# A chunked linear-attention scan: running sums placed behind the step, value rows copied on the chip, weight pieces offered twice as often

## The chip, the cores and the metric

The kernel runs on one core of a Trainium2 chip. A core has five engines that run their own instruction streams in order and meet only at semaphores: PE (matrix products, with PEld loading the stationary operand), DVE (vector), ACT (activation functions and scaled copies), POOL (GpSimd) and SP (which here only issues DMA transfers). The metric is the device time of one execution in microseconds (us): for the kernel before, the median of three runs is 2766.99 us (2765.91 to 2770.10).

## The reference, cut to what matters

Two layers of a hybrid backbone. Each layer has modulation vectors (`silu(c) @ w_ada`), three parallel token mixers merged by sigmoid gates, and a gated feed-forward part. The change touches the first mixer (a delta-rule scan in two directions, six heads of 64), and the modulation and gate products that are computed beside it.

```python
def _rwkv_step(S, inp):
    r, w, k, v, a, b = inp
    sa = jnp.einsum('bhij,bhj->bhi', S, a)
    S = S * w[:, :, None, :] + sa[..., None] * b[:, :, None, :] + v[..., None] * k[:, :, None, :]
    return S, jnp.einsum('bhij,bhj->bhi', S, r)
...
mod_lat = (jax.nn.silu(c) @ w_ada[l] + b_ada[l])[:, None, :]
...
gA, gB, gC = jnp.split(jax.nn.sigmoid(gate_u), N_BRANCH, axis=-1)
m = gA * (yA @ p['w_branch_a']) + gB * (yB @ p['w_branch_b']) + gC * (yC @ p['w_branch_c'])
```

## The kernel before, in words

Weights are split into a high and a low float32r part (L183 on ACT, L184 on DVE) and each dense product is three passes over them. Each layer goes through: projections for the scan (`rwkv_project`), the scan (`rwkv_scan`), the other mixers (Fourier and attention, `mixers`), the merge and the feed-forward part. In the profile the scan of layer 0 lies at about 205 to 600 us, the mixers of layer 0 behind it to about 890 us, and the scan of layer 1 at about 1780 to 2120 us.

The scan is cut into 12 chunks of 64 tokens for both directions at once. A chunk n has a **preparation** and a **step**.

- The preparation, `prep(n)`, reads the chunk's tile `X` (four transfers, L991 and L992, from `rwx` and `rws`), makes the running sum of the log decays (`cum`, L1006, one DVE instruction), five exponentials of it on ACT (L1013 to L1017), the scaled operands `BK` and `AR` (L1024 to L1030), their products (`f`), the masks (`MA`, `MY`), and then inverts a triangular matrix in eight rounds (`inverse`, tiles `i...`, L1087 to L1139): each round is a PE product followed by DVE or ACT work that the next product waits for. Its result is `TT`. At the end GpSimd copies `AR` into `MA` (L1060).
- The step, `step(n)`, is the serial part: product with the state `SV`, copy `Rh` (L1153, DVE), product with `TT`, copy into `UV` (L1160 on DVE, L1161 on ACT), product with `Bn`, `St` (L1173) and the new state `SV` (L1175, one half on DVE and the other on GpSimd). The outputs `y` are products of `SV` and `UV`.
- `SV` and `UV` both hold, in one half of their partitions, the value rows of the chunk. Before, both are filled from the array `v_tok` in memory by four transfers each (L978 for `SV`, three buffers; L999 for `UV`, three buffers). `X` has two buffers (`XB`).

SP issues all these transfers and the weight tiles (`wr`, three buffers in rotation, L191 for gate weights, L245 for modulation weights) in one order; a transfer whose buffer is still in use holds back all that stand behind it.

**Background work.** The products of the gates (`L688`, bank `w`, one buffer; ACT reads them out at L693) and the modulation parts (`ada_part`, L258: eight small products per part in four pieces of 512 KB of weights, then L261, four transposes at L265 and a reduction at L268) are not part of the scan. `Background.after` is called behind each small product chain of the scan and issues some of that work there, counted in planned microseconds (`due`). While the scan runs (`side`), a modulation part can be advanced by one piece (`aside`, bank `a`, its next piece loaded ahead) at each point where the gate stream yields 0.0: at the end of each of its two parts (512 and 256 columns), and, where `MID[l]` is true, also halfway through each. What is left of layer 0's modulation parts when its scan ends is put between the remaining gates (`mix`) and runs in the mixers phase from the `fill` calls, in the bank `w` that the gates use, without loading ahead.

The order of instructions on each engine is fixed when the program is built: a list scheduler with a simulated timeline places each instruction when its inputs are ready by its own estimate; `tc.issue_after(x)` keeps an instruction behind instruction x in it.

Of the kernel before, what the change touches and what calls it, by code (L numbers as in the profile page):

```python
# [11 lines left out]
F32 = mybir.dt.float32  # L12
# [3 lines left out]
ALU = mybir.AluOpType  # L16
# [49 lines left out]
MFILL, AFILL = 2.5, 0.3  # L66
FIRST = ((12, 2.0), (8, 3.0))
MORE = False
XB, UB = 2, 3
MID = (False, True)  # L70
FILL = (1.0, 0.8)
PRE = (12.0, 24.0)
CUTS = dict(
# [9 lines left out]
def hybrid_backbone_kernel(ctx: ExitStack, tc: tile.TileContext, A, out, dbg=None):  # L83
    nc = tc.nc
    V, S, P, TE = nc.vector, nc.scalar, nc.gpsimd, nc.tensor
# [21 lines left out]
    def pss(tag="s"):  # L107
        return banks[tag].tile([128, 512], F32, tag=tag, name=tag)
# [6 lines left out]
    def C(name, n=None):  # L115
        o = COFF[name]
        w = dict(CCOLS)[name] if n is None else n
        return cst[:, o:o + w]
# [45 lines left out]
    v_tok = dram.tile([T, 2, 3, 64], F32, name="v_tok")  # L164
# [506 lines left out]
    def gate_part(l, it, W, hH, hL, streams, pool):  # L671
# [3 lines left out]
        for a, b in streams:  # L675
# [8 lines left out]
            else:  # L684
                WH, WL = W
                for n, (w, X) in enumerate(((WH, hH), (WL, hH), (WH, hL))):
                    for k in range(8):
                        TE.matmul(ps, lhsT=w[:, k, :], rhs=X[k][:, a:b], start=(k == 0 and n == 0), stop=(k == 7 and n == 2))  # L688
                        if (n, k) != (2, 7):
                            yield (b - a) / 2400  # L690
                        if MID[l] and (n, k) == (1, 3):
                            yield 0.0
# [249 lines left out]
    def rwkv_scan(l, last, pool, fill):  # L942

        hs = (slice(0, 64), slice(64, 128))
# [27 lines left out]

        def state(n):

            SV = pool.tile([128, 2, 6, 64], F32, tag="SV", name="SV", bufs=3)
            for d, c in enumerate(chunks(n)):
                for p in range(2):
                    nc.sync.dma_start(out=SV[hs[1 - p], p, 3 * d:3 * d + 3, :], in_=v_tok[c * 64:c * 64 + 64, p])  # L978
            return SV


        def chunks(n):
            return (8 + n, 11 - n) if n < 4 else (n - 4, 11 - n)

        def load(n):
            ch = chunks(n)
            need_y = not (last and n < 4)
            X = pool.tile([128, 5, 2, 192], F32, tag="X", name="X", bufs=XB)
            for d in range(2):
                w = 2 if need_y else 1  # L990
                nc.sync.dma_start(out=X[:, 2:5, d], in_=rwx[d, ch[d]].rearrange("p w c t -> p w (c t)"))  # L991
                nc.sync.dma_start(out=X[:, 0:w, d], in_=rws[ch[d], :, 0:w].rearrange("p w c t -> p w (c t)"))  # L992
            return X

        def values(n):
            UV = pool.tile([128, 2, 6, 64], F32, tag="UV", name="UV", bufs=UB)
            for d, c in enumerate(chunks(n)):
                for p in range(2):
                    nc.sync.dma_start(out=UV[hs[1 - p], p, 3 * d:3 * d + 3, :], in_=v_tok[c * 64:c * 64 + 64, p])  # L999
            return UV  # L1000

        def prep(n, X):
            need_y = not (last and n < 4)
            w = 128 if need_y else 64
            cum = pool.tile([128, 2, 192], F32, tag="cum", name="cum", bufs=1)
            V.tensor_tensor_scan(out=cum.rearrange("p d x -> p (d x)"), data0=C("seq"), data1=X[:, 4].rearrange("p d x -> p (d x)"),  # L1006
                                 initial=0.0, op0=ALU.mult, op1=ALU.add)
            G = Gs[n % 2]
            I = X[:, 4]
            gc = pool.tile([128, 6], F32, tag="gc", name="gc", bufs=4)  # L1010
            c = 0.5 * DECAY_C
# [129 lines left out]

        def step(n, SV, UV, pk):
            AR, MY, Bn, TT, gc, WA = pk
# [3 lines left out]
            ps, run = pss("st"), Run()  # L1147
            for u in range(6):
                for p in range(2):
                    i = run(TE.matmul, ps[hs[p], u * 64:(u + 1) * 64], lhsT=WA[:, p, u, :], rhs=SV[:, p, u, :], start=True, stop=True)  # L1150
            fill(i)
            Rh = pool.tile([128, 384], F32, tag="Rh", name="Rh", bufs=1)
            V.tensor_copy(Rh, ps[:, 0:384])  # L1153
            ps, run = pss("st"), Run()
            for u in range(6):
                for p in range(2):
# [5 lines left out]
            if n < 11:  # L1162
                gb = gc.unsqueeze(2).to_broadcast([128, 6, 64])
                Sg = pool.tile([128, 6, 64], F32, tag="Sg", name="Sg", bufs=1)
                for p in range(2):
                    P.tensor_tensor(out=Sg[hs[p]], in0=SV[hs[p], p], in1=gb[hs[p]], op=ALU.mult)
                ps, run = pss("st"), Run()
# [8 lines left out]
            if need_y:  # L1176
                ps = pss("st")
# [3 lines left out]
                for u in range(6):  # L1181
                    for p in range(2):
                        o = ps[hs[p], u * 64:(u + 1) * 64]
                        m1 = run(TE.matmul, o, lhsT=SV[:, p, u, :], rhs=AR[:, u, 2 - 2 * p, :], start=True, stop=False)
                        for q in prev:
# [12 lines left out]
                    S.dma_start(out=y_dram[d, :, :, ch[d] * 64:ch[d] * 64 + 64].rearrange("c p t -> p c t"), in_=yt[:, d])  # L1198
            return SV1

        ld = [load(0), load(1)]
        SV = state(0)
        for p in range(2):
            P.memset(SV[hs[p], p], 0.0)
        uv = [values(0), values(1)]
        pk = [prep(0, ld[0])]
        ld.append(load(2))
        uv.append(values(2))
        pk.append(prep(1, ld[1]))
        for n in range(12):  # L1210
            if n + 3 < 12:
                ld.append(load(n + 3))
            SV = step(n, SV, uv[n], pk[n])
            if n + 3 < 12:
                uv.append(values(n + 3))
            if n + 2 < 12:
                pk.append(prep(n + 2, ld[n + 2]))

    def rwkv_out(l, last, pool, fill):

# [39 lines left out]
    for k in range(KD):  # L1260
        x = xp.tile([128, T], F32, name=f"x{k}")
# [24 lines left out]
    for l in range(DEPTH):  # L1286
# [8 lines left out]
        with ExitStack():  # L1295
# [28 lines left out]
            def fill(us=MFILL):  # L1324
                bg.run(us)
# [27 lines left out]
        with ExitStack() as es:  # L1353
            for c in range(8):
                x = xp.tile([128, T], F32, name=f"x{c}")
# [4 lines left out]
            with ExitStack() as e2:  # L1360
                tp = near(e2, l, f"mt{l}")
                for c in range(8):
                    acc = None
                    for x in (2, 1, 0):
                        t = tp.tile([128, T], F32, tag=f"t{x}", name=f"t{x}", bufs=2)
                        nc.sync.dma_start(out=t[:, ar], in_=t_dram[x, c][:, ar])
                        ps = dense(A[("w_ba", "w_bb", "w_bc")[x]][l, c], len(yX[x][0]), yX[x][0], yX[x][1], streams)
# [169 lines left out]
```

## Time and profile before

| | |
|---|---|
| median of three runs | 2766.99 us |
| the profiled execution | 2763.33 us |
| its span, first to last instruction | 2761.6 us |
| PE busy | 2580.6 us (93%) |
| DVE, ACT, POOL busy | 1474.6, 1076.6, 209.7 us |
| mean granted TensorE clock | 0.975 |
| largest DMA queue (SP's) | 278.66 MB, 32.5% of 16 engines' span |

A busy PE is not a PE at its peak, but where it is idle or at the lower clock, time is lost that nothing else can give back, since PE has work left over in every stage. So the stages are read by PE's idle time and granted clock first, then by what PE waited for there, and then by what that engine waited for.

### The profile page before, as it was taken

The numbers are of one execution on the slowest core, as the hardware profiler recorded it, in microseconds if no ns is written. First come the engines' busy times: TensorE is split into PE (matmuls) and PEld (weight loads), VectorE is DVE, ScalarE is ACT, GpSimd is POOL, SyncE is SP. The second block draws the span as 40 slices with busy tenths as digits, with TensorE's granted clock in tenths as the row PEclk, the third lists the DMA queues.
The fourth block names the chain that finished last, engine by engine and source line by source line (L and its number), as shares of the span: only waits on it lengthen the run. The fifth ranks groups of instructions, "written<-read, shape, count | busy, mean of one in ns | idle before, by whom it ended". The sixth has DMA issues, their size and how long they took to land.

```text
span 2761.6 us, 56820 instructions
## 1 busy us (share of the span) xinstructions
PE 2580.6 (93%) x24016; PEld 2062.0 (75%) x24016; DVE 1474.6 (53%) x2965; ACT 1076.6 (39%) x1914; POOL 209.7 (8%) x268
## 2 busy tenths in 40 slices
PE   6998998997899999999999999998898899899999
PEld 4866776775776887888888877666666668878778
DVE  6444545434446765445354564445564768755455
ACT  4353333332445253222222344544343564533333
POOL 0121121100010000000000001302220000000000
PEclk9999998998999999999999999999999999999999
DMA  6365443356441641221212254765444417333334
GB/s 264 93 176 173 132 137 108 119 190 205 133 139 42 183 122 48 60 69 55 68 49 74 61 170 109 234 196 154 134 134 148 130 50 220 108 92 90 98 95 123
DMA packets 168947, 344.18 MB, mean 125 GB/s; under 512 B 33618, under 2 KB 84436, under 8 KB 168692
## 3 DMA queue, kind: packets, MB, share of 16 engines
q1 hardware_dynamic: 132532, 278.66, 32.5%
q0 software_dynamic: 10944, 36.58, 5.0%
q10 hardware_dynamic: 25216, 25.30, 2.7%
q8 instruction: 190, 3.11, 0.5%
q14 instruction: 65, 0.53, 0.1%
HBM read 278.60 MB, written 61.87 MB: 123 GB/s over the span
## 4 chain that ended last, share of the span: by engine, by line
PE 67%; DMA 5%; DVE 5%; ACT 2%; issue 2%; SPq 1%; ACTq 0%; POOL 0%; DVEq 0%; POOLq 0%
PE mm L220 44%; PE w L688 9%; PE mm L567 2%; DMA wr<-in_w_ada 2%; PE r L595 2%; PE s L584 1%; PE st L957 1%; PE i L957 1%; DVE wl L184 1%; PE mm L394 1%; DMA X<-rwx 1%; PE a L258 1%; PE w L258 1%; PE s L871 1%; DMA raw<-m_dram 1%
## 5 line engine op out<-in xcount | busy, mean ns | idle before, releaser
L183 ACT ACTIVATE wh<-wr 128x1024 fp32r<-128x1024 f32 (+4 forms) x334 | 302.0, 906 | 373.7 <-PE mm L220 272.1
L184 DVE TENSOR_TENSOR wl<-wr,wh 128x1024 fp32r<-128x1024 f32 (+3 forms) x332 | 342.8, 1034 | 59.4 <-ACT wh L183 56.9
L220 PE MATMUL mm<-fH,wh 128*128 128x512 f32 (+1 forms) x1072 | 223.9, 357 | 10.3 <-DVE ab L232 7.2
L231 DVE SCALAR_TENSOR_TENSOR ab<-mm,prm,ab 128x511 f32<-128x511 f32 (+1 forms) x132 | 86.8, 658 | 262.3 <-ACT ab L229 262.3
L220 PE MATMUL mm<-fH,wl 128*128 128x512 f32 (+1 forms) x1072 | 220.3, 353 | 0.0
L220 PE MATMUL mm<-fL,wh 128*128 128x512 f32 (+1 forms) x1072 | 219.6, 352 | 0.0
L688 PE MATMUL w<-hH,wh 128*128 128x512 f32 (+1 forms) x760 | 189.0, 385 | 22.4 <-ACT gt L693 21.0
L220 PEld LDWEIGHTS mm<-fH,wh 128*128 128x128 f32 x1072 | 178.1, 191 | 41.7 <-issue 6.4
L220 PEld LDWEIGHTS mm<-fH,wl 128*128 128x128 f32 x1072 | 175.8, 189 | 29.6
L220 PEld LDWEIGHTS mm<-fL,wh 128*128 128x128 f32 x1072 | 175.4, 188 | 29.5
L688 PE MATMUL w<-hL,wh 128*128 128x512 f32 (+1 forms) x760 | 184.4, 374 | 0.0
L220 PE MATMUL mm<-gH,wh 128*128 128x512 f32 (+1 forms) x568 | 174.5, 346 | 10.0 <-ACT wh L183 4.4
L688 PE MATMUL w<-hH,wl 128*128 128x512 f32 (+1 forms) x760 | 174.6, 364 | 2.7 <-issue 2.7
L220 PE MATMUL mm<-gH,wl 128*128 128x512 f32 (+1 forms) x568 | 175.4, 348 | 1.1 <-DVE wl L184 0.9
L688 PEld LDWEIGHTS w<-hH,wh 128*128 128x128 f32 x760 | 128.6, 197 | 63.2 <-ACT gt L693 29.6
L1255 DVE SCALAR_TENSOR_TENSOR x<-mm,mod,x 128x256 f32<-128x256 f32 (+1 forms) x136 | 80.1, 607 | 173.1 <-PE mm L220 172.2
L220 PE MATMUL mm<-gL,wh 128*128 128x512 f32 (+1 forms) x568 | 171.5, 343 | 0.0
L229 ACT ACTIVATE ab<-mm,prm 128x768 f32<-128x768 f32 (+1 forms) x88 | 69.9, 795 | 217.9 <-PE mm L220 217.9
L688 PEld LDWEIGHTS w<-hL,wh 128*128 128x128 f32 x760 | 128.6, 195 | 25.1 <-issue 4.1
L688 PEld LDWEIGHTS w<-hH,wl 128*128 128x128 f32 x760 | 128.1, 192 | 24.7 <-issue 3.3
L220 PEld LDWEIGHTS mm<-gH,wh 128*128 128x128 f32 x568 | 97.1, 188 | 29.6 <-ACT wh L183 10.4
L693 ACT ACTIVATE gt<-w 128x512 f32<-128x512 f32 x99 | 51.4, 519 | 161.7 <-PE w L688 143.6
(387 smaller groups left out, 4649.8 us busy)
## 6 DMA issues: line engine op xcount, KB each, us to landing
wr<-in_w_up SPq DMA_DIRECT2D x88, 512.0 KB
wr<-in_w_ada SPq DMA_DIRECT2D x80, 512.0 KB
wr<-in_w_g SPq DMA_DIRECT2D x48, 512.0 KB
wr<-in_w_out SPq DMA_DIRECT2D x32, 512.0 KB
wr<-in_w_dn SPq DMA_DIRECT2D x48, 320.0 KB
X<-rwx SPq DMA_DIRECT2D x48, 288.0 KB
wr<-in_w_rw SPq DMA_DIRECT2D x24, 512.0 KB
wr<-in_w_dn SPq DMA_DIRECT2D x32, 384.0 KB
```

The source lines that it names most:

```text
L183: S.activation(out=H, in_=raw, func=AF.Copy)
L184: e.tensor_tensor(out=L, in0=raw, in1=H.bitcast(F32), op=ALU.subtract)
L220: TE.matmul(ps[:, a:b], lhsT=W[:, k, :], rhs=X[k][:, a:b], start=(k == 0 and n == 0), stop=(k == kt - 1 and n == 2))
L229: S.activation(out=o[:, a:b], in_=ps[:, a:b], func=AF.Identity, scale=w[1])
L231: V.scalar_tensor_tensor(out=o[:, a + 1:b], in0=ps[:, a:b - 1], scalar=w[0], in1=o[:, a + 1:b], op0=ALU.mult, op1=ALU.add)
L258: TE.matmul(ps[32 * i:32 * i + 32], lhsT=cs32[:, k, :], rhs=w[:, k - k0], start=(k < 4), stop=(k >= 4))
L567: TE.matmul(ps[:, a:b], lhsT=qT[:, h, t * 128:(t + 1) * 128], rhs=kT[:, h, a:b], start=True, stop=True)
L595: TE.matmul(po[64 * p:64 * p + 64, 0:128], lhsT=Vn[:, j, h * 64:(h + 1) * 64], rhs=pts[p][:, j * 128:(j + 1) * 128], start=(j == kts[0]), ...
L688: TE.matmul(ps, lhsT=w[:, k, :], rhs=X[k][:, a:b], start=(k == 0 and n == 0), stop=(k == 7 and n == 2))
L693: S.activation(out=t[:, a:b], in_=ps, func=AF.Tanh if it[0] == "g" else AF.Copy, scale=0.5 if it[0] == "g" else 1.0)
L957: self.i = f(*a, **k)
L1255: V.scalar_tensor_tensor(out=x[:, a:b], in0=ps[:, a:b], scalar=mod[l][:, j, c, s:s + 1], in1=x[:, a:b], op0=ALU.mult, op1=ALU.add)
```

## The change

Four edits in the scan and two numbers.

- `cum` of chunk n+2 is issued behind `Rh` of step n (`issue_after`); the sums of chunks 0 and 1 stay free.
- `UV` gets its value rows from `SV` by two GpSimd copies per chunk (64 partitions x 384 elements) in place of four transfers; it has two buffers in place of three.
- `SV` has four buffers in place of three.
- `MID` is true for layer 0 too, as it was for layer 1.

```diff
-XB, UB = 2, 3
-MID = (False, True)
+XB, UB = 2, 2
+MID = (True, True)
...
-            SV = pool.tile([128, 2, 6, 64], F32, tag="SV", name="SV", bufs=3)
+            SV = pool.tile([128, 2, 6, 64], F32, tag="SV", name="SV", bufs=4)
...
-        def values(n):
+        def values(SV):
             UV = pool.tile([128, 2, 6, 64], F32, tag="UV", name="UV", bufs=UB)
-            for d, c in enumerate(chunks(n)):
-                for p in range(2):
-                    nc.sync.dma_start(out=UV[hs[1 - p], p, 3 * d:3 * d + 3, :], in_=v_tok[c * 64:c * 64 + 64, p])
+            for p in range(2):
+                P.tensor_copy(UV[hs[1 - p], p], SV[hs[1 - p], p])
             return UV
...
-        def prep(n, X):
+        def prep(n, X, behind=None):
...
-            V.tensor_tensor_scan(out=cum.rearrange("p d x -> p (d x)"), data0=C("seq"), data1=X[:, 4].rearrange("p d x -> p (d x)"),
-                                 initial=0.0, op0=ALU.mult, op1=ALU.add)
+            with tc.issue_after(behind.ins) if behind else ExitStack():
+                V.tensor_tensor_scan(out=cum.rearrange("p d x -> p (d x)"), data0=C("seq"), data1=X[:, 4].rearrange("p d x -> p (d x)"),
+                                     initial=0.0, op0=ALU.mult, op1=ALU.add)
...
-            V.tensor_copy(Rh, ps[:, 0:384])
+            rhs[0] = V.tensor_copy(Rh, ps[:, 0:384])
...
-        uv = [values(0), values(1)]
...
-            SV = step(n, SV, uv[n], pk[n])
-            if n + 3 < 12:
-                uv.append(values(n + 3))
+            SV = step(n, SV, values(SV), pk[n])
             if n + 2 < 12:
-                pk.append(prep(n + 2, ld[n + 2]))
+                pk.append(prep(n + 2, ld[n + 2], rhs[0]))
```

Three places in the new order, each before and after. The first is DVE in layer 0 about the fourth step (chunk 3, `Rh_4109` before and `Rh_4113` after). Before, the running sum `cum_5113` there is that of chunk 7, and it stands ahead of the step:

```order
L1101 TENSOR_TENSOR iX_3848<-i0_3853,iDX_3805 128x192
L1006 SCALAR_TENSOR_TENSOR cum_5113<-cst_75,X_4535 128x384
L1103 TENSOR_TENSOR iNX_3806<-i0_3898,iX_3848 128x6x32
L1137 COPY TT0_1870<-i1_3597 32x3x32
L1105 STREAM_TRANSPOSE iXt_3849<-iNX_3806 128x192
L1137 COPY TT0_1870<-i1_3597 32x3x32
L1027 TENSOR_TENSOR AR0_1877<-X_4077,G0_1873 128x6x64
L1153 COPY Rh_4109<-st_4087 128x384
```

After, the sum behind the same step is that of chunk 5 (`cum_4188`), and the operands `BK` and `AR` that are made from it follow at once, in part ahead of the step's next copy, `UV`:

```order
L1153 COPY Rh_4113<-st_4095 128x384
L1006 SCALAR_TENSOR_TENSOR cum_4188<-cst_75,X_3609 128x384
L1090 TENSOR_TENSOR iD0_3800<-iF_3795,cst_75 128x192
L1093 TENSOR_TENSOR iE_3802<-iF_3795,cst_75 128x192
L1091 STREAM_TRANSPOSE iDt_3801<-iD0_3800 128x192
L1092 TENSOR_TENSOR iDX_3803<-iD0_3800,cst_75 128x6x32
L1024 TENSOR_TENSOR BK_4196<-X_3609 128x6x64
L1026 TENSOR_TENSOR BK_4196<-X_3609 128x6x64
L1160 COPY UV_4087<-st_4115 64x384
```

So the sums stand two chunks ahead of the step in place of four.

The second place is SP at the start of layer 0's scan, where the tiles `X` of chunks 0 and 1 and the first value rows are fetched. Before:

```order
L991 DMA X_1889<-rwx_114 128x3x192
L992 DMA X_1889<-rws_113 128x2x192
L991 DMA X_1889<-rwx_114 128x3x192
L245 DMA wr_2020<-in_w_ada 128x1024
L992 DMA X_1889<-rws_113 128x2x192
L991 DMA X_1894<-rwx_114 128x3x192
L992 DMA X_1894<-rws_113 128x2x192
L991 DMA X_1894<-rwx_114 128x3x192
L992 DMA X_1894<-rws_113 128x2x192
L978 DMA SV_1899<-v_tok_115 64x192 x4
L999 DMA UV_1906<-v_tok_115 64x192 x3
```

After, with the same names but for their numbers:

```order
L991 DMA X_1893<-rwx_114 128x3x192
L992 DMA X_1893<-rws_113 128x2x192
L991 DMA X_1893<-rwx_114 128x3x192
L245 DMA wr_1844<-in_w_ada 128x1024
L191 DMA wr_1849<-in_w_m 128x1024
L245 DMA wr_2115<-in_w_ada 128x1024
L992 DMA X_1893<-rws_113 128x2x192
L991 DMA X_1898<-rwx_114 128x3x192
L992 DMA X_1898<-rws_113 128x2x192
L991 DMA X_1898<-rwx_114 128x3x192
L992 DMA X_1898<-rws_113 128x2x192
L978 DMA SV_1903<-v_tok_115 64x192 x2
```

The transfers into `UV` are gone, and three weight tiles in place of one stand ahead of the last part of the first `X`.

The third place is PE in the mixers phase of layer 0, behind a gate's last product of 256 columns. Before, a modulation part (L258, its transposes L265) stands between this gate and the next:

```order
L688 MATMUL w<-hL_156,wh 128x256
L416 MATMUL s<-cst,sq 128x1 x6
L258 MATMUL w<-wr,cs_102 32x512 x8
L265 MATMUL w<-cst,row 128x128 x4
L688 MATMUL w<-hH_141,wh 128x512
```

After, the attention's own products (L394) stand there, and the next gate comes without a part between:

```order
L688 MATMUL w<-hL_155,wh 128x256
L688 MATMUL w<-hL_156,wh 128x256
L394 MATMUL mm<-mh,cH 128x384
L394 MATMUL mm<-mh,cL 128x384
L394 MATMUL mm<-ml,cH 128x384
L394 MATMUL mm<-mh,cH 128x384
```

Counted over the whole order of PE: of the 12 modulation parts in the background of layer 0, 6 run in the scan and 6 in the mixers phase before; after, 10 and 2, and the mixers phase has 9 gates in place of 8. Layer 1 has all its 8 parts in its scan in both.

## Rows read from the trace of the kernel before

**Rows 1.** The page: busy time, share and instructions of each engine.
```profile
PE 2580.6 (93%) x24016; PEld 2062.0 (75%) x24016; DVE 1474.6 (53%) x2965; ACT 1076.6 (39%) x1914; POOL 209.7 (8%) x268
```
**Rows 2.** Busy time by stretch: length, engines (instructions), PE clock, DMA share, GB/s.
```profile
205.00:260.00 55.00, 45.66 (x415) 33.95 (x418) 22.28 (x47) 17.82 (x47) 11.28 (x20) 0.88 0.61 181
260.00:480.00 220.00, 196.81 (x4353) 156.41 (x4344) 113.24 (x273) 81.49 (x211) 38.24 (x44) 0.97 0.44 131
480.00:580.00 100.00, 98.81 (x2112) 77.66 (x2109) 42.99 (x107) 34.32 (x82) 16.93 (x20) 0.97 0.35 109
674.00:780.00 106.00, 90.45 (x514) 70.56 (x514) 43.35 (x125) 44.02 (x67) 4.42 (x9) 0.90 0.45 143
1800.00:2040.00 240.00, 217.57 (x4609) 159.14 (x4609) 131.81 (x310) 98.57 (x247) 39.02 (x45) 0.96 0.52 160
2040.00:2117.00 77.00, 72.99 (x1675) 53.88 (x1669) 37.41 (x92) 27.24 (x64) 16.57 (x18) 1.00 0.43 124
```
**Rows 3.** Who PE waited for, 260 to 480 us: total, times, longest.
```profile
PE w L688 <- ACT gt L693: 9.4, 2, 7.0
PE i L954 <- DVE iX L1101: 4.1, 2, 3.3
```
**Rows 4.** Instructions in order of time, 346 to 359 us: SP, DVE, ACT, PE.
```profile
346.73 2.90 SPq L999 DMA_DIRECT2D UV<-v_tok  x4
349.93 0.55 SPq L991 DMA_DIRECT2D X<-rwx  x1
...
356.31 0.96 DVE L1006 TENSOR_TENSOR_SCAN cum<-cst,X 128x384 f32<-128x384 f32 x1 [2.65 <-DMA X<-rwx]
...
357.35 0.36 ACT L1013 ACTIVATE X<-cum 128x192 f32<-128x192 f32 x1 [5.99 <-DVE cum L1006]
...
358.40 0.21 PE L954 MATMUL i<-iX,iQ 32*32 32x32 f32 x1 [2.60 <-ACT iQ L1125]
```
**Rows 5.** Line 1006, whole span: DVE idle before it, until what; total, times.
```profile
  DMA X<-rwx: 84.5, 19
```
**Rows 6.** Who SP's queue waited for, 200 to 610 us: total, times, longest.
```profile
SPq L978 <- PE st L957: 55.3, 7, 12.9
```
**Rows 7.** Lines 999, 1060, 1027: count, duration min/median/max in ns, first and last start.
```profile
L999 SPq DMA_DIRECT2D UV<-v_tok x96: 444/593/1980, 230.2 to 2060.9; - x96
...
L1060 POOL COPY MA<-AR x48: 496/505/722, 275.1 to 2112.3; 64x384 f32<-64x384 f32 x48
...
L1027 DVE TENSOR_TENSOR AR<-X,G x24: 526/550/1335, 228.7 to 2041.7; 128x384 f32<-128x384 f32 x24
```
**Rows 8.** Start of layer 0's scan, in order of time: SP, PE.
```profile
208.52 0.59 SPq L991 DMA_DIRECT2D X<-rwx  x1
223.49 0.34 SPq L245 DMA_DIRECT2D wr<-in_w_ada  x1
...
245.13 0.25 PE L954 MATMUL i<-iD,iDt 32*32 32x32 f32 x1 [4.43 <-DVE iDt L1091]
```
**Rows 9.** Who PE waited for, 674 to 780 us: total, times, longest.
```profile
PE w L258 <- DMA wr<-in_w_ada: 10.7, 4, 4.5
```
**Rows 10.** PE in order of time: last pieces of two modulation parts, mixers of layer 0.
```profile
710.97 1.92 PE L258 MATMUL w<-wr,cs 128*32 128x512 f32 x4 [2.54 <-DMA wr<-in_w_ada]
...
743.25 1.05 PE L258 MATMUL w<-wr,cs 128*32 128x512 f32 x4 [1.96 <-DMA wr<-in_w_ada]
```
**Rows 11.** Who PE waited for, 1800 to 2117 us: total, times, longest.
```profile
PE w L688 <- ACT gt L693: 6.0, 3, 5.7
PE a L258 <- DMA wr<-in_w_ada: 4.4, 3, 2.5
```
**Rows 12.** Lines 1153, 1025, 1139 in layer 1's scan: as in Rows 7.
```profile
L1153 DVE COPY Rh<-st x12: 545/557/558, 1856.2 to 2117.2; 128x384 f32<-128x384 f32 x12
L1025 ACT ACTIVATE BK<-BK x12: 515/524/527, 1792.1 to 2063.1; 128x384 f32<-128x384 f32 x12
L1139 ACT ACTIVATE TT<-i x24: 241/242/243, 1850.0 to 2113.5; 32x96 f32<-32x96 f32 x24
```

More of the change, by code (lines that the diff above doesn't have):

```diff
@@ L1199, in step @@
             return SV1
+        rhs = [None]
         ld = [load(0), load(1)]
@@ L1204, in rwkv_scan @@
             P.memset(SV[hs[p], p], 0.0)
-        uv = [values(0), values(1)]
         pk = [prep(0, ld[0])]
         ld.append(load(2))
-        uv.append(values(2))
         pk.append(prep(1, ld[1]))
```

## The prediction

> **What bounds the kernel now.** I read the page first: PE is busy for 2580.6 of 2761.6 us [rows 1], so about 181 us of idle PE is all that any rearrangement can win, beside what the clock takes. The change leaves PE's products as they are and moves them, so the question is where in the three stages it touches PE stands idle or slow. The view of busy time by stretch gives that [rows 2]. In the middle of layer 0's scan (260 to 480 us) PE is idle for 220 - 196.8 = 23.2 us; in the 100 us behind it, where no running sum is left to make, for 1.2 us. In layer 1 it is idle for 240 - 217.6 = 22.4 us up to 2040 us, and for 77 - 73.0 = 4.0 us behind. In the mixers of layer 0, from 674 to 780 us, it is idle for 106 - 90.5 = 15.5 us and the granted clock is 0.90, that is, part of this stretch runs at 1.2 and not 2.4 GHz.
>
> Then the waits. In layer 0's scan PE's longest waits are for ACT to empty the gate bank (9.4 us in two waits, one of 7.0) and for DVE and ACT inside the inversion [rows 3]. These engines are not busy (DVE 113 of 220 us, [rows 2]), so something holds them in their order. Rows in order of time show what: SP spends 2.90 us on four `UV` transfers, and only then issues `X`, at 349.93; DVE has the running sum of that `X` next in its order and stands idle for 2.65 us until 356.31; ACT waits for the sum 5.99 us; the small ACT copy that PE needs stands behind, and PE is idle for 2.60 us [rows 4]. DVE waits for `X` in this way 19 times, 84.5 us in all [rows 5]. SP itself was held back before: its `SV` transfers wait 55.3 us for PE's products of an older step, because `SV` has three buffers [rows 6].
>
> **The change part by part.** I sum against the profiled execution, 2763.3 us.
>
> *Running sums behind the step, four `SV` buffers, no `UV` transfers.* The order shows the sum two chunks ahead of the step in place of four. Its `X` then takes a buffer that came free about two steps earlier, while SP loses 96 transfers of 0.59 us each (57 us of issue, [rows 7]) and the wait on the third `SV` buffer. So `X` has landed when the sum comes up, and the 84.5 us of DVE idle should all but go. PE gets back only its own part. From both sides: nothing, if other waits take their place; at most the idle down to the quiet rates, 23.2 - 2.2 x 1.2 = 20.6 us in layer 0 and 22.4 - 240 x 4.0 / 77 = 9.9 us in layer 1 [rows 2]. The quiet stretches have fewer preparations in flight, so I stay below: 15 us and 8 us. The clock of these stretches is 0.97 and 0.96, at most 6.6 and 9.6 us of full-speed time; the quiet stretch of layer 1 has 1.00, that of layer 0 only 0.97. I take 2 and 4 us. Scans: -29 us.
>
> *What this costs.* Behind `Rh` DVE now has the sum (0.96 us), two `BK` and two `AR` products, with a wait for ACT's exponentials, partly ahead of the step's `UV` copy. That is some 4 to 5 us on the step's serial path where before it was spread; it is covered as long as PE has gate products between, which the order still places there. With a chunk less of lead the inversion's rounds stand closer together, and each round too close costs PE a fraction of a microsecond. Not shown in any row: between 0 and the whole gain; I take 3 us.
>
> *Copies by GpSimd.* 48 copies of 64 x 384, like line 1060's at 0.505 us [rows 7]: 24 us of an engine that is busy for 209.7 us [rows 1]. They need no time on the path, since the values of chunk n+2 are copied while step n+1 is still to come. But DVE's `AR` product, 550 ns at the median, took up to 1335 ns [rows 7], 0.79 us more, and GpSimd is the engine that works at the same time on the same tiles. Between 0 and 48 x 0.79 = 38 us of DVE time; most copies will meet no such product, and DVE has as much idle as busy time, so I take 2 us for PE.
>
> Beside that stands a rule of the Trainium skill, "SBUF — State Buffer", section "Who interferes with whom": a DVE instruction with two SBUF inputs and a GpSimd instruction that reads SBUF exclude each other, and the later one blocks until the earlier ends. It speaks against the copies, and this trace agrees with it as far as the 550 and 1335 ns go. By it a copy would hold such a DVE instruction for its own 0.5 us at most, 24 us of DVE time for all 48, within the bounds above; the sum stays.
>
> *Modulation parts halfway through layer 0's gates.* By the order, 4 of 6 parts leave the mixers phase for the scan and one gate goes the other way. PE's work is the same in sum. In the mixers a part is loaded piece by piece without loading ahead: the four parts between 674 and 780 us cost four waits for the last piece, 10.7 us [rows 9]. The stall also costs clock: the last piece took 1.92 us behind one such wait and 1.05 us behind another [rows 10], a factor of 1.83, near that of the two levels, and 0.90 over 106 us is at most 10.6 us of full-speed time [rows 2]. The four parts that leave are these, as the order has the gates at their places without them; the first two, at 604 to 655 us, stay. Between 0 (if attention's own chain sets the pace there) and 15.5 + 10.6 = 26 us; I take the 10.7 us and 3 us of clock. Mixers: -14 us.
>
> In the scan a part is loaded one piece ahead. Layer 1 shows the price: 8 parts, 4.4 us of waits [rows 11], so 0.55 us each, 2 us for four more.
>
> *The start of layer 0's scan.* Here the change adds to a queue. Before, SP stood from 208.5 to 223.5 us in front of one modulation tile, which waits for a buffer, and the rest of the first `X` came behind it [rows 8]; PE then waited 4.43 us for the first inversion [rows 8] and was idle for 55 - 45.7 = 9.3 us in this stretch [rows 2]. After, three tiles stand there, each waiting for a buffer that PE's products release. Two more issues are 0.7 us and two more tiles of 512 KB at the 181 GB/s of this stretch [rows 2] 5.8 us, if nothing overlaps; from 1 to 7 us, I take 3.
>
> Sum: -29 + 3 + 2 - 14 + 2 + 3 = -33 us, 2730.3 us for an execution like the profiled one. The median of the runs lies 3.7 us above that one, so the forecast is 2767.0 - 33 = **2734 us**.
>
> **The rivals.**
>
> *Only the mixers gain.* The scan's stalls change places (the `UV` copy behind `BK`, rounds that stand too close) and the scans come out even; 2767 - 14 = 2753 us. For it: PE waits in the inversion without any transfer, 4.1 us [rows 3]. Against it: behind the last sum PE is hardly idle [rows 2].
>
> *Nothing.* Gains of the scan and the mixers are eaten by the start and by the second part of the mixers, where the gates that move in meet attention's own waits: 2767 us. For it: DVE's 84.5 us cost PE only a fraction even now.
>
> *Slower: the preparation becomes the chain.* In layer 1 the step's period is (2117.2 - 1856.2) / 11 = 23.7 us [rows 12]. The last chunk's operands were ready at 2063.1 and its step followed at 2117.2: 54 us, and about 2.5 us more from the sum. With the sum bound behind `Rh` of step n, all of that has to fit before `Rh` of step n+2, into 47.5 us. If the preparation kept its 56.5 us, the period would be 28.3 us, and ten steps 46 us longer; in layer 0, at a period of some 27 us, about 15 us. It decides from the point where a preparation is longer than two periods. Half of the 61 us, less the mixers' 14, gives +17: 2784 us. For it: the numbers above. Against it: these 54 us are mostly waiting, for the gate products between the rounds and for DVE standing at later sums, and the order has the rounds closer together.
>
> **How the numbers follow.** Forecast 0.62, with 2712 to 2752 as its own range (half the scan's gain missing and no clock gained, or all bounds reached in the scans); only the mixers 0.16; nothing 0.09; slower 0.13. A change under 0.2%, 5.5 us, can't be told from none here. Faster: 0.62 + 0.16 = 0.78. The range of 2708 to 2768 leaves out the slower case and about 0.05 below.
>
> **What would show it.** Right: DVE's idle before line 1006 falls from 84.5 us to under 15; no transfer at line 999; PE's idle in the scans' middle stretches falls to about 8 and 14 us; six waits for modulation pieces in the mixers become two places, and the clock from 674 us on is near 1. Wrong: PE waiting for inversion rounds in many places of 1 to 2 us, or steps of layer 1 more than 25 us apart (the preparation bounds), or a first inversion later than 250 us with PE idle before it, or attention's products waiting for DVE where the modulation parts were.

## The result and the profile after

The changed kernel takes 2721.35 us (median of four runs, 2718.23 to 2723.43) against 2767.47 us (2765.91 to 2770.10) for the kernel before; the ratio is 0.9828, with a 95% interval of 0.9813 to 0.9842. That is 46 us less; forecast were 33 us and 2734 us, with a range of 2708 to 2768. The profiled execution of the changed kernel is its slowest, 2723.43 us, and so shows 40 us of the 46.

The page: engine, busy time, share of the span, instructions [rows 1].

```profile
PE 2581.3 (95%) x24016; PEld 2062.2 (76%) x24016; DVE 1467.6 (54%) x2965; ACT 1075.3 (40%) x1914; POOL 234.5 (9%) x316
```

PE is as long busy as before (2580.6), so all 40 us are idle time of PE: 2761.6 - 2580.6 = 181.0 before, 2721.6 - 2581.3 = 140.3 after. In these two executions the clock gave nothing in sum.

Busy time by stretch, as in [rows 2]; the mixers' stretch begins as far behind the scan's end as before, and the two of layer 1 are set 33.5 us earlier, as the first `Rh` of that layer is.

```profile
205.00:260.00 55.00, 49.01 (x474) 37.12 (x463) 18.86 (x46) 16.51 (x40) 13.05 (x25) 0.88 0.65 205
260.00:480.00 220.00, 212.55 (x4587) 161.59 (x4585) 115.30 (x286) 83.73 (x218) 50.41 (x64) 1.00 0.51 154
480.00:580.00 100.00, 97.86 (x1955) 73.80 (x1955) 41.30 (x101) 35.24 (x88) 15.92 (x21) 1.00 0.38 117
663.00:769.00 106.00, 99.70 (x596) 88.91 (x597) 44.20 (x109) 49.08 (x78) 8.08 (x15) 0.97 0.30 93
1766.50:2006.50 240.00, 230.41 (x4846) 169.53 (x4845) 134.07 (x318) 100.36 (x249) 52.62 (x68) 0.99 0.52 159
2006.50:2083.50 77.00, 71.62 (x1489) 51.53 (x1488) 38.16 (x97) 27.62 (x68) 15.01 (x19) 0.98 0.37 109
```

PE's idle in the middle of layer 0's scan falls from 23.2 to 7.5 us, in layer 1's from 22.4 to 9.6 us, in the later mixers from 15.5 to 6.3 us, at the start from 9.3 to 6.0 us.

Cut at marks that both traces have (first running sum of a layer, first `Rh`, last product of the scan, next product of line 220), in us:

| stage | length before, after | PE idle before, after |
|---|---|---|
| up to the first sum | 214.4, 215.4 | 26.5, 26.9 |
| layer 0: first sum to first `Rh` | 70.0, 60.9 | 11.0, 6.0 |
| layer 0: first `Rh` to the scan's end | 305.2, 302.5 | 22.8, 9.6 |
| layer 0: mixers | 294.2, 272.7 | 30.7, 21.3 |
| dense part, to layer 1's first sum | 905.7, 909.1 | 23.7, 23.7 |
| layer 1: first sum to first `Rh` | 66.6, 61.9 | 3.5, 0.3 |
| layer 1: first `Rh` to the scan's end | 270.0, 265.1 | 23.8, 14.9 |
| layer 1: mixers | 144.6, 141.3 | 18.9, 17.2 |
| the rest | 490.8, 492.4 | 19.9, 20.4 |

Who PE waited for from 260 to 480 us of the changed kernel (total, times, longest), where before stood 9.4 us for the gate bank [rows 3]:

```profile
PE i L957 <- issue: 4.3, 5, 1.5
PE i L954 <- issue: 0.7, 1, 0.7
...
PE w L688 <- ACT gt L693: 0.5, 1, 0.5
PE f L954 <- DVE AR L1027: 0.4, 1, 0.4
```

DVE's running sums over the whole span (duration, first and last start; then its idle before them), where 84.5 us stood [rows 5]:

```profile
L1006 DVE TENSOR_TENSOR_SCAN cum<-cst,X x24: 935/948/958, 215.4 to 2032.7; 128x384 f32<-128x384 f32 x24
...
  DMA X<-rwx: 9.2, 3
```

Nine tenths of DVE's stand at `X` are gone. What is left are the first sums of the two layers, in order of time:

```profile
215.39 0.96 DVE L1006 TENSOR_TENSOR_SCAN cum<-cst,X 128x384 f32<-128x384 f32 x1 [6.59 <-DMA X<-rwx]
...
1760.77 0.96 DVE L1006 TENSOR_TENSOR_SCAN cum<-cst,X 128x384 f32<-128x384 f32 x1 [2.02 <-DMA X<-rwx]
...
1767.92 0.96 DVE L1006 TENSOR_TENSOR_SCAN cum<-cst,X 128x384 f32<-128x384 f32 x1 [0.58 <-DMA X<-rwx]
```

No sum behind a step waits for `X` any more. Before, the same three first sums took 6.82, 12.52 and 0.47 us, and the other 64.7 us in 16 places lay inside the scans.

In the mixers the pieces of two modulation parts are left (590 to 680 us, who PE waited for; from 663 us on none is, where [rows 9] had 10.7 us):

```profile
PE w L258 <- DMA wr<-in_w_ada: 10.7, 4, 5.4
PE mm L394 <- ACT Vn L491: 2.5, 1, 2.5
```

### The profile page after: what moved, and what is told of

Read it like the earlier page. It is cut to its first block, busy times and chain, and to the rows that moved or that the text cites. A ratio compares the mean times of both kernels' runs of the same rounds, so it can differ in the third digit from the quotient of the medians.

```text
span 2721.6 us, 56800 instructions
## 1 busy us (share of the span) xinstructions
PE 2581.3 (95%) x24016; PEld 2062.2 (76%) x24016; DVE 1467.6 (54%) x2965; ACT 1075.3 (40%) x1914; POOL 234.5 (9%) x316
## 4 chain that ended last, share of the span: by engine, by line
PE 86%; DVE 5%; DMA 4%; ACT 3%; issue 2%; SPq 0%; ACTq 0%; DVEq 0%; POOL 0%; POOLq 0%
PE mm L220 47%; PE w L688 15%; PE st L957 3%; PE i L957 3%; PE mm L567 2%; PE a L258 2%; PE r L595 2%; PE mm L394 2%; PE s L584 1%; DMA wr<-in_w_ada 1%; PE s L871 1%; PE f L957 1%; PE i L954 1%; DVE wl L184 1%; PE f L954 1%
## 5 line engine op out<-in xcount | busy, mean ns | idle before, releaser
L220 PE MATMUL mm<-fH,wh 128*128 128x512 f32 (+1 forms) x1072 | 225.0, 358 | 10.5 <-DVE ab L232 7.4
L220 PEld LDWEIGHTS mm<-gH,wl 128*128 128x128 f32 x568 | 97.3, 188 | 17.5 <-DVE wl L184 3.7
```

What stands on the lines that cost most here:

```text
L220: TE.matmul(ps[:, a:b], lhsT=W[:, k, :], rhs=X[k][:, a:b], start=(k == 0 and n == 0), stop=(k == kt - 1 and n == 2))
```

## The experiments

The change has three parts that can be had apart: the **sums** behind `Rh`, the **copies** by GpSimd (with two `UV` and four `SV` buffers), and the **parts** at half of layer 0's gate streams. The runs give all eight combinations. The median of the kernel before on the chips of these runs was 2763.5 to 2766.9 us; the ratio to it is what can be compared. DVE's idle is that before the running sums on transfers of `X`.

| kernel | median us | ratio (95% interval) | DVE's idle us |
|---|---|---|---|
| parts | 2755.28 | 0.9965 (0.9948 to 0.9982) | 71.6 |
| sums | 2733.54 | 0.9880 (0.9861 to 0.9899) | 20.1 |
| copies | 2767.57 | 1.0008 (0.9989 to 1.0026) | 78.9 |
| copies and parts | 2762.54 | 0.9991 (0.9978 to 1.0004) | 64.7 |
| sums and copies | 2726.20 | 0.9854 (0.9831 to 0.9877) | 8.7 |
| sums and parts | 2719.70 | 0.9838 (0.9820 to 0.9855) | 10.5 |
| all three (the change) | 2721.35 | 0.9828 (0.9813 to 0.9842) | 9.2 |

**Parts alone.**

```diff
-MID = (False, True)
+MID = (True, True)
```

> The kernel before with MID true for layer 0 as its only edit. By the theory that the change's gains add up place by place, the mixers of layer 0 lose four of their six modulation parts and the waits for their last pieces, and their stage gets about 20 us shorter, while the scan of layer 0 gets 5 to 8 us longer by the parts it now carries: 2767 - 14 = 2753 us, DVE's idle before the running sums as before (84 us). By the rival, that the parts find room only where the scan's stalls are gone, the scan gets longer by nearly what the mixers lose: 2762 to 2768 us.

2755.3 us, as the first theory had it. The mixers are 25.5 us shorter (268.7 for 294.2), in part because PE's work on four parts moved out of them; the first `Rh` to the scan's end of layer 0 5.9 us longer (311.1) and the way to the first `Rh` 2.2 us longer; layer 1's scan with its start was 6 to 7 us longer in this execution, with PE idle for 30.9 us in place of 27.3, though the edit doesn't touch it.

**Sums alone.**

```diff
+            with tc.issue_after(behind.ins) if behind else ExitStack():
...
+            rhs[0] = V.tensor_copy(Rh, ps[:, 0:384])
...
+                pk.append(prep(n + 2, ld[n + 2], rhs[0]))
```

> The kernel before with the running sum of chunk n+2 behind Rh of step n as its only edit; the value rows still come by transfers, SV has three buffers. By the theory that the order of the sums makes DVE wait, DVE's idle before line 1006 falls from 84 us to under 20, PE's idle in both scans falls by 15 to 20 us and the time is about 2746 us. By the rival, that SP's queue (the UV transfers and the wait for the third SV buffer) makes DVE wait, the idle before line 1006 stays over 40 us and the time over 2758 us. If the first step comes 8 us earlier here as it does with the whole change, the order is the cause of that too.

2733.5 us: the order is the cause, and more of it than expected. The sums' row of this kernel (its lines stand one lower), with the 96 transfers still in SP's queue and three `SV` buffers:

```profile
L1007 DVE TENSOR_TENSOR_SCAN cum<-cst,X x24: 947/948/958, 215.8 to 2039.0; 128x384 f32<-128x384 f32 x24
...
  DMA X<-rwx: 20.1, 3
```

The 20.1 us are again the first sums of the layers alone (7.52, 12.25 and 0.28 us). The queue still has all its transfers, and no sum behind a step waits. Of the 27.0 us between the two profiled executions 17.6 lie in layer 0's scan with its start, 4.6 in layer 1's and 7.7 in the mixers; the rest took 2.9 us more. PE's idle in the two scans falls by 22.7 us, for the 15 to 20 expected.

The first `Rh` comes 5.3 us sooner behind the first sum (64.7 for 70.0 us), so more than half of the start's 9.1 us comes from the order too.

**Copies alone.**

```diff
-XB, UB = 2, 3
+XB, UB = 2, 2
...
-            SV = pool.tile([128, 2, 6, 64], F32, tag="SV", name="SV", bufs=3)
+            SV = pool.tile([128, 2, 6, 64], F32, tag="SV", name="SV", bufs=4)
...
+            for p in range(2):
+                P.tensor_copy(UV[hs[1 - p], p], SV[hs[1 - p], p])
```

> The kernel before with the value rows of UV copied by GpSimd, two UV and four SV buffers, and no other edit. By the theory of the order, DVE still stands at sums four chunks ahead whose X has no free buffer: 2760 to 2767 us, idle before line 1006 over 60 us. By the rival of SP's queue: 2745 us and under 30 us. DVE's products of line 1027 stay at a median of 0.55 us if it is the neighbourhood of GpSimd's half of line 1030 that lengthens them after the change, and rise towards 1.2 us if the copies lengthen them. The first step comes some 8 us earlier, at 276 us, if the transfers into UV had held the start.

2767.6 us, no gain. Without transfers of `UV`, and with a fourth `SV` buffer, DVE stands at the sums as before, and its `AR` product keeps its 0.55 us (two rows of this kernel, its lines one higher: the sums with DVE's idle before them, and `AR`):

```profile
L1005 DVE TENSOR_TENSOR_SCAN cum<-cst,X x24: 943/958/960, 215.1 to 2039.5; 128x384 f32<-128x384 f32 x24
...
  DMA X<-rwx: 78.9, 22
...
L1026 DVE TENSOR_TENSOR AR<-X,G x24: 534/556/1331, 230.7 to 2054.2; 128x384 f32<-128x384 f32 x24
```

The start is not shorter (73.7 us from the first sum to the first `Rh`). So the transfers into `UV` and the third `SV` buffer, taken alone, were not what held the sums. That does not clear the queue as a whole. From 200 to 610 us SP's wait at the `SV` transfers fell from 55.3 to 31.7 us, but its waits with weight tiles for the modulation parts' products rose (57.8 to 78.4 us at line 245, 36.7 to 60.4 at line 191), and so did that of `X` for its own two buffers (6.8 to 20.8 us). Which of these made the `X` of an early sum late was not separated: no kernel with three `X` buffers was run.

**Sums and copies.** The change with `MID = (False, True)`.

> The changed kernel with MID false for layer 0 again (sums behind the step and copies by GpSimd, but the modulation parts as before). By adding up: 2721 + 14 = 2735 us, with PE's idle in the scans as low as with the whole change and the mixers as long as before, about 294 us. By the rival, that the parts gain only together with the sums, it gives up 20 us or more: 2741 us or above.

2726.2 us, better than adding up, and 7 us below the sums alone, by runs that don't overlap (2725.3 to 2727.8 against 2729.4 to 2736.5). Of the 9.9 us between the two profiled executions 7.2 lie in the mixers, where no copy runs. PE's idle in the scans is low as expected (11.1 us in layer 0's steps), but the mixers are not as long as before: 279.3 us with the same six parts in them. There the waits for pieces are already less (569.6 to 848.9 us, its mixers, where the kernel before has 21.3 us in eight waits):

```profile
PE w L258 <- DMA wr<-in_w_ada: 13.5, 7, 5.0
```

So the mixers win 14.9 us without the edit meant for them: 6.4 us of idle (24.4 for 30.7) and 8.5 us of busy PE for the same parts and gates, at a granted clock of 0.97 for 0.94. The scheduler draws up the mixers anew when the scan changes; which of its moves brings the pieces sooner wasn't tested.

**Sums and parts.** Value rows by transfers, three `SV` buffers: the first two diffs together.

> The kernel before with the sums behind the step and MID true for layer 0; the value rows of UV still come by transfers and SV has three buffers. The three parts alone gave 31.6 us (sums), 9.8 us (parts) and no gain (copies); sums and copies gave 38.9 us, the whole 45 to 46 us. If parts and copies each add what they add on top of the others (5 and 7 us), this one comes to 2727 us, DVE's idle before the running sum about 20 us, PE's idle in the mixers of layer 0 about 21 us. If the parts only shorten waits that the copies shorten too, it comes as low as 2722 us; if the parts need the free queue of SP, it stays at 2733 us.

2719.7 us, the lower of the forecasts: without the copies it takes what the whole change takes.

**Copies and parts.** The change without the sums' order.

> The changed kernel with the sums free again (copies by GpSimd, four SV buffers and MID for layer 0, but no order behind Rh). If copies and parts do nothing for DVE's stand at early sums, DVE idles 70 us or more before them and the time is that of the parts alone, 2755 us, within 4 us. If the copies give the 7 us beside the parts that they gave beside the sums, 2748 us.

2762.5 us. DVE's idle, 64.7 us, is a little under the 70 expected, the time is above both forecasts: without the order the copies add nothing to the parts, and may take something from them. The times of this kernel scatter over 13 us (2755.5 to 2768.9). Against it the whole change shows what the order is worth beside the others: 0.9991 to 0.9828, 45 us.

**Three `SV` buffers in the changed kernel.**

```diff
-            SV = pool.tile([128, 2, 6, 64], F32, tag="SV", name="SV", bufs=4)
+            SV = pool.tile([128, 2, 6, 64], F32, tag="SV", name="SV", bufs=3)
```

> The changed kernel with three SV buffers in place of four. By the theory of SP's queue the transfers into SV wait for PE's products of an older step again, some 40 us in layer 0's scan, X comes late for a few sums, DVE's idle before line 1006 rises from 9 us to 20 or more as it was with the transfers, and the time to about 2726 us. By the rival, that with the sums two chunks ahead nothing behind SV in the queue is needed soon, the wait is there and the time stays at 2721 us, within 2 us.

2722.7 us, ratio 0.9845 (0.9829 to 0.9860), DVE's idle 9.3 us: the fourth buffer shows no effect. SP's wait at the `SV` transfers, 55.3 us before [rows 6], is 17.7 us with three buffers and 16.0 us with four. With the sums alone, three buffers and all transfers, it is 12.2 us, with the copies and four buffers alone 31.7. So the order of the sums shortens it most.

**AR without GpSimd.** In the changed kernel DVE's `AR` product of line 1027 rose from a median of 0.55 to 1.24 us:

```profile
L1027 DVE TENSOR_TENSOR AR<-X,G x24: 540/1235/1303, 235.9 to 2035.3; 128x384 f32<-128x384 f32 x24
```

In order of time (start, duration), DVE in layer 0's scan:

```profile
337.50 0.55 DVE L1026 TENSOR_TENSOR BK<-X 128x384 f32<-128x384 f32 x1
337.96 1.29 DVE L1027 TENSOR_TENSOR AR<-X,G 128x384 f32<-128x384 f32 x1
339.17 0.54 DVE L1030 TENSOR_TENSOR AR<-X,G 64x384 f32<-64x384 f32 x1
```

GpSimd in the same microseconds:

```profile
337.58 1.26 POOL L1030 TENSOR_TENSOR AR<-X,G 64x384 f32<-64x384 f32 x1 [8.88 <-DVE BK L1024]
```

Beside it runs not a copy but GpSimd's half of the product of line 1030. This edit gives that half to DVE:

```diff
-                for p, e in enumerate((V, P)):
+                for p, e in enumerate((V, V)):
                     e.tensor_tensor(out=u4(AR[:, :, 2 - 2 * p, :])[hs[p]], ...
```

> The changed kernel with the second half of AR (line 1030's half on GpSimd) made by DVE too, so that no GpSimd product with two inputs runs beside DVE's AR product. If it is GpSimd's half that lengthens that product, all 24 of line 1027 but one or two take 0.55 us (14 us in sum in place of 23.8 us), PE's waits for AR (7.0 us before the first f products in three places) fall under 3 us, and the time is 2717 to 2720 us. The rival is that the copies into UV lengthen it: then the median of line 1027 stays above 1 us. A third: DVE's 20 more products of 0.55 us stand on the step's path and cost more than they give, 2722 to 2728 us.

2712.3 us, ratio 0.9805 (0.9789 to 0.9821). The product is back at 0.55 us with all 48 copies still there (line 1027, and who waited for line 1030):

```profile
L1027 DVE TENSOR_TENSOR AR<-X,G x24: 509/551/1181, 235.5 to 2021.2; 128x384 f32<-128x384 f32 x24
...
  PE f L954: 8.2, 4
```

So GpSimd's half lengthens it. But PE's waits for `AR` did not fall (7.5 us in the changed kernel, 8.2 here), so the step from there to the time is refuted. The time was lower than every expectation; its interval overlaps that of the changed kernel at the edge, and where 9 us would come from isn't shown.

**All parts in the scan.**

```diff
-                        if MID[l] and (n, k) == (1, 3):
+                        if MID[l] and (n, k) in (((0, 3), (1, 3), (2, 3)) if l == 0 else ((1, 3),)):
```

> The changed kernel with three places in place of one within each stream of layer 0's gates at which a modulation piece may go, so that all 12 parts of layer 0's background run in its scan, none in its mixers, and the mixers have 12 gates in place of 9. If a part costs in the mixers what its waits and the clock behind them take (10.7 us and, at 0.82 and 0.78 over 60 us, some 12 us of full-speed time), the mixers get about 15 to 20 us shorter by the idle and the clock, the time 2705 to 2712 us. If the gates that move into the mixers run where attention's own work fills PE, and the scan gets longer by what it takes over, as the parts edit showed on top of the others (5 us for four parts), the time is 2717 to 2721 us. If the transfers of the pieces take SP's queue from X, DVE's idle before the sums rises over 20 us and it is slower than 2723 us.

2709.1 us, ratio 0.9809 (0.9790 to 0.9828); a second, single run gave 2713.0 us. The mixers are 260.6 us long, 12.1 less, with 11.2 us of idle PE in place of 21.3 and no wait for a piece; the scan is less than 1 us longer. Two parts' 11.4 us of PE left the mixers and 12.2 us of gates came, so what fell there is idle and clock. The first 90 us of the mixers in the changed kernel (columns as in [rows 2]):

```profile
578.90:608.90 30.00, 28.05 (x168) 21.26 (x169) 15.38 (x40) 10.74 (x21) 0.00 (x0) 1.00 0.84 284
608.90:638.90 30.00, 21.91 (x111) 15.23 (x109) 12.29 (x37) 7.76 (x17) 0.10 (x1) 0.82 0.67 220
638.90:668.90 30.00, 24.32 (x120) 20.96 (x121) 19.58 (x54) 13.79 (x22) 0.00 (x0) 0.78 0.54 178
```

The same 90 us in this one:

```profile
578.80:608.80 30.00, 26.90 (x144) 21.90 (x143) 13.48 (x32) 9.03 (x17) 0.00 (x0) 0.89 0.60 199
608.80:638.80 30.00, 29.25 (x168) 24.18 (x167) 16.78 (x48) 11.75 (x24) 0.10 (x1) 1.00 0.58 204
638.80:668.80 30.00, 28.62 (x167) 25.30 (x167) 17.88 (x43) 14.32 (x22) 0.00 (x0) 1.00 0.61 203
```

PE's idle falls and the clock rises where the two parts stood, and the time is as the first theory had it, with somewhat less taken from the mixers. DVE's idle before the sums is 19.9 us, short of the third, and again only at the layers' first sums (7.32 and 12.57 us). The second run's expectation:

> A second look at the changed kernel with three places for modulation pieces in each stream of layer 0's gates, in the company of the next two: 2709 us, within 4 us.

**Both, with and without the copies.** The last two edits together in the changed kernel:

> The changed kernel with both edits that were faster than it alone: AR's second half on DVE (2712.3 us alone) and three places for modulation pieces in layer 0 (2709.1 us alone). If they save in different places (the AR products in both scans, the parts in layer 0's mixers) the savings of 9 and 12 us add: 2700 us. If both only take up the same slack of layer 0's scan, 2706 to 2709 us.

and together with sums and parts but the transfers of `UV` and three `SV` buffers:

> The same two edits without the copies: the value rows of UV come by transfers again, with three SV buffers. Sums and parts without the copies took 2719.7 us against 2721.4 us with them, so if the copies are worth nothing once the sums and parts are there, this one takes what the last one takes, 2700 us, within 3 us. If the larger number of pieces in the scan needs the queue free of the UV transfers, it is 5 us or more slower than the last one, and DVE's idle before the sums is larger by 10 us or more.

2711.4 us (0.9814, 0.9798 to 0.9830) and 2710.7 us (0.9808, 0.9792 to 0.9823). The first is above both of its forecasts: the two savings don't add. The second takes what the first takes: beside the sums and the parts the copies are again worth nothing. Each of these four kernels is 9 to 12 us below the changed kernel by its median; by ratio the difference is 0.14 to 0.23%, with intervals that overlap. Against the kernel before they are clear.

## Why the prediction was right, and where its sizes were off

**The sums.** The mechanism holds: `X` has landed when the sum comes up, and DVE's 84.5 us shrink to 9.2. All that is left are the first sums of the layers. But the prediction gave the credit to three edits together, and argued with SP's 57 us of issue and the wait for the third `SV` buffer. The runs show that the order alone does it (20.1 us of idle and 0.9880), and that these two reliefs of SP alone do nothing (78.9 us and 1.0008). In the sums' run the queue still held the 96 transfers, and no sum behind a step waited. So the sums were called for too soon; whether their `X` was then late for the queue or for its two buffers stays open.

In sizes: idle of PE fell by 13.2 us in layer 0's steps (15 forecast, less 3 for the rounds) and by 12.1 us in layer 1's scan with its start (8 forecast). The 3 us for closer rounds were not seen as waits in layer 0, where the longest is 1.5 us.

**The start: the step that failed.** The prediction added 3 us, and the first `Rh` came 8.1 us sooner; behind the first sum it came 9.1 us sooner, with 5.0 us less idle of PE on the way, and the rest is PE's work that now stands elsewhere. It counted SP's queue alone. That cost is real: GpSimd's first half of `AR` started at 233.3 where it was 228.7, once the rest of `X` was there. DVE's first `AR` product started at 235.9 where it was 228.7 [rows 7], behind a weight split (line 184) that had waited 6.59 us for ACT. But it also had to count DVE's order there: before, the sums of chunks 2, 3 and 4 stood ahead of the first step, and two of them waited for `X`. In the kernel before, DVE's sums from 240 us to the first `Rh`:

```profile
243.38 0.96 DVE L1006 TENSOR_TENSOR_SCAN cum<-cst,X 128x384 f32<-128x384 f32 x1 [2.30 <-issue]
...
251.94 0.96 DVE L1006 TENSOR_TENSOR_SCAN cum<-cst,X 128x384 f32<-128x384 f32 x1 [4.19 <-DMA X<-rwx]
...
268.67 0.96 DVE L1006 TENSOR_TENSOR_SCAN cum<-cst,X 128x384 f32<-128x384 f32 x1 [2.43 <-DMA X<-rwx]
```

The changed kernel, `Rh` and the first sum behind it; none stands between 237.8 and this:

```profile
276.33 0.56 DVE L1153 COPY Rh<-st 128x384 f32<-128x384 f32 x1 [0.47 <-PE st L957]
...
277.93 0.95 DVE L1006 TENSOR_TENSOR_SCAN cum<-cst,X 128x384 f32<-128x384 f32 x1
```

So 8.9 us of idle and three sums went from the way to the first step. The first inversion's product was at 243.89 for 245.13 [rows 8] although `AR` was later. The sums' run has most of this (64.7 us), the copies' none (73.7).

**The mixers.** -14 was forecast, as idle and clock: 10.7 us of waits and 3 us. The stage is 21.5 us shorter, but most of what isn't idle there is PE's work that moved into the scan. PE on the modulation parts' products and on the gates', before and then after (the stage, length, PE busy, clock, DMA share, GB/s):

```profile
589.60:883.80 294.20, 23.57 (x96) 0.94 0.44 143
589.60:883.80 294.20, 88.58 (x456) 0.94 0.44 143
...
578.90:851.60 272.70, 9.29 (x32) 0.95 0.38 125
578.90:851.60 272.70, 95.57 (x504) 0.95 0.38 125
```

With the parts' transposes (5.7 us before, 2.1 after) that is 10.9 us of work less. So 10.6 us compare with the forecast, 9.4 of them idle: somewhat less than the 14, not more. The four parts' waits went as forecast, from 674 us on all of them, and the clock there went from 0.90 to 0.97; over the whole stage it is only 0.95 for 0.94, with 0.82 and 0.78 where the two parts that are left wait. Nor are the 10.6 us the parts' alone: with sums and copies the mixers won 14.9 us with all six parts in place. The stage was taken as fixed but for the parts, and that the term comes out near its size is in part luck.

**The clock.** 9 us were forecast as clock, and PE's busy time is unchanged in the profiled pair. In layer 0's scan the granted clock did rise from 0.97 to 1.00 in both stretches, as forecast, and PE's busy time in layer 0's scan and mixers fell by 5.5 us; the dense part, layer 1 and the rest took 6.2 us more with the same products. The pair is not an even one. The kernel before was profiled at a mean granted clock of 0.975, where its other executions on the three chips of the experiments have 0.970 to 0.977; the changed one was profiled at 0.980, the lowest of its four (0.980 to 0.982). And over the kernels of all runs, with the same 24016 products, the page's busy time is 2573.1 to 2589.1 us. A clock term of 9 us is neither shown nor refuted by this pair.

In the sum two misses work against each other: the clock, 9 us that the pair doesn't show, and the start, where 3 us were added and PE's idle fell by 5.0. That they nearly cancel is luck.

**Copies by GpSimd.** 2 us were forecast as their cost. Alone, or beside the sums and the parts, nothing clear was measured either way; beside the sums alone they come with 7 us less, most of it in the mixers, where none of them runs. The reason given for the range was wrong: the 1335 ns of [rows 7] were GpSimd's half of `AR`, not a neighbour that the copies would resemble. With the sums in one place that half runs beside DVE's product in most chunks, and so the median rose to 1235 ns, and without the copies too (1291 in the sums' run). It costs DVE nothing in sum, since before it was DVE's own half of line 1030 that was lengthened. That half in the kernel before:

```profile
L1030 DVE TENSOR_TENSOR AR<-X,G x20: 542/1167/1364, 229.2 to 2057.9; 64x384 f32<-64x384 f32 x20
```

And in the changed kernel:

```profile
L1030 DVE TENSOR_TENSOR AR<-X,G x20: 540/542/850, 236.3 to 2036.6; 64x384 f32<-64x384 f32 x20
```

All `AR` products of DVE take 37.9 us before and 35.0 after.

**The rivals.** That only the mixers gain is refuted by the sums' run, nothing by the interval. The slower one, preparation as the chain, misread a row: it put the last sum about 2.5 us ahead of the last operands at 2063.1, and that sum stood 41 us ahead of them, at 2022.3:

```profile
L1006 DVE TENSOR_TENSOR_SCAN cum<-cst,X x24: 950/958/959, 214.4 to 2022.3; 128x384 f32<-128x384 f32 x24
```

From its sum to its `Rh` a chunk took 90 to 116 us in layer 1 before and takes 37 to 56 us now, past the first two chunks; the last sum is at 2032.7, the last `Rh` at 2078.9, 46.2 us. So most of the time before was standing, as the prediction's own argument against this rival had it, and the steps did not move apart. The period is (2078.9 - 1822.7) / 11 = 23.3 us, for 23.7 [rows 12]:

```profile
L1153 DVE COPY Rh<-st x12: 541/556/558, 1822.7 to 2078.9; 128x384 f32<-128x384 f32 x12
```

## What to carry to other kernels

An engine that runs in order should not be asked for work before its input can be there: a look-ahead of four chunks over two buffers made DVE stand at 16 of 24 sums, beside the first ones of each layer, and with it all that was queued behind them; moving that one instruction back by two chunks was worth 33 us alone and 45 us beside the other parts. Where a moved instruction leaves a serial path, look at the first step too, here three sums and 8.9 us of DVE's idle came off the way to it. One kernel per part told the causes apart that the diff had bundled: the transfers taken out and the buffer added with them were worth nothing alone or beside the other two, and only beside the sums alone did the kernel with them take 7 us less. And where work moves between stages, the change of a stage's length is not its gain: take the idle and the clock, and count the products.

## What the runs showed of the hardware

When GpSimd's product with two inputs and a DVE product of the same kind overlap, both come out long: 1.26 us on GpSimd (0.93 at the least) and 1.29 us on DVE (0.55 alone), and DVE's ends 0.41 us behind GpSimd's, less than its own 0.55 us. The Trainium skill's rule ("SBUF — State Buffer", section "Who interferes with whom"), that such instructions exclude each other and the later waits, agrees with this to within 0.14 us, and GpSimd's own 0.33 us more lie beside the end of DVE's `BK` product, which began 0.08 us ahead of it. The 48 copies, which read one input, met few such products: beside them nine DVE instructions took over 0.1 us more than the median of the same instruction away from GpSimd's work, 2.4 us together, of the 24 us that were the rule's bound in the prediction.
